# Attention on one Trainium2 core: value products split by key halves, scores tiled by two heads and 64 tokens

## The chip, the cores and the metric

The kernel runs on one core of a Trainium2 chip. The core has five engines that run side by side: TensorE (PE: matrix products; its weight loads are listed apart as PEld), VectorE (DVE), ScalarE (ACT), GpSimd (POOL) and SyncE (SP, which here only issues transfers). They meet in two on-chip memories: SBUF, with 128 partitions, and PSUM, where TensorE writes its results, in eight banks of 512 float32 numbers per partition. The metric is the device time of one execution in microseconds (us); lower is better.

## What is computed

Two layers over 1024 tokens of width 1024, in float32. The first is a gated MLP that mixes tokens in chunks of 128; it ends at about 640 us of the profile and is not touched. The second is sliding-window attention:

```python
logits = jnp.einsum('btkgd,bskd->bkgts', qb, kb).astype(jnp.float32) + alibi
valid = in_window & ((start - BLOCK + c) >= 0)        # 0 <= t - s < 128
logits = jnp.where(valid, logits, -jnp.inf)
m = jnp.maximum(jnp.max(logits, axis=-1), sink)
p = jnp.exp(logits - m[..., None])
denom = jnp.sum(p, axis=-1) + jnp.exp(sink - m)
o = jnp.einsum('bkgts,bskd->btkgd', p.astype(vb.dtype), vb).astype(jnp.float32)
o = o / denom.transpose(0, 3, 1, 2)[..., None]
y = out * jax.nn.silu(z)
return y @ w_out
```

There are 16 query heads of 64 channels in 4 groups; a group shares one key/value head. Tokens come in 8 blocks of 128. A token sees itself and the 127 tokens before it, so a block of queries needs the keys of its own block up to the token, and those of the block before it from the token on. Every token of a block thus has 128 keys with weight, spread over 256 keys.

## The kernel before

*Products in float32 from parts.* Long products use a split: a number is held as a rounded high part and a remainder (`split`, line 104; `mm3`, line 168), and three products (lines 169 to 171) stand for one. Scores and projections use this format (float32r). The value products and the transposes use plain float32 operands.

*A unit.* `Unit` (line 1041) is one block b of 128 queries for one pair p of key/value heads, so 8 query heads. There are 16 units. `scores(gp)` (line 1048) does half of a unit: two banks, one per head of the pair (`par`), each with two query heads side by side. For every query head and `par` it multiplies the query block (128 channels by 128 tokens; the high part stands in one half of the partitions, the remainder in the other) with the 256 keys, once with `kh` and once with `kl`: eight matmuls of 256 columns (line 1069). In block 0 there is no previous block and they have 128 columns. VectorE then folds the two key blocks into one: where the mask `mrg` (key index over token index) holds, the score of the current block is overwritten by that of the previous one (line 1074, 2 x 128 columns). It adds the slope bias and takes the maximum, with the sink as a lower bound, in one instruction per head (line 1080). ScalarE takes the exponential with its sum (line 1084). `normalise` divides. `transposes` (line 1092) turns the weights into keys by tokens with eight transposes (line 1097), ScalarE copies them to the tile `pc` (line 1098), and GpSimd cuts `pc` into the part of the previous block, `pp`, and that of the current block, `pc` (lines 1101, 1102).

*Value products.* `values` (line 1104) computes, for each `par`, 64 output channels by 512 columns (4 heads of 128 tokens): one matmul with the current block's values (`vt`, 128 keys by 64 channels, line 1116) and one with the previous block's (line 1118), added in the same bank `o`. The two `par` use the two column halves of the TensorE array. VectorE multiplies the bank with the gate (line 1122), and `split` writes the result over the queries, as the operand of the output projection.

*The order of work.* The attention is laid out by hand in `attn` (line 1125). In step i it issues `scores(0)` of unit i, `values` of unit i-2, two portions of filler, `transposes` of unit i-1, `scores(1)` and `normalise` of unit i, and two portions of filler. The filler (`more`) is a generator of other matmul work: key/value, query and gate projections of the second half of the tokens (`kv_phase`, `q_phase`, `z_phase`) during the first half's attention, and output projections (`out_b0`, `out_b1`) during the second's. Each engine runs its own instructions in the order given; semaphores are placed where a result of another engine is needed.

*Buffers.* PSUM has two rings of four banks. The ring "s" serves scores (two banks per group), `o` (one bank) and the transposes (two). Each use waits until the use four places earlier has been read out. `pc` and `pp` share a ring of two tiles in SBUF (tag "xt"). Small constants (`bias`, `mrg`, `qsc`, `snk`) are loaded by SP at line 945 on, and the sinks are negated by VectorE (line 957).

Of the kernel before, what the change touches and what calls it, by code (L numbers as in the profile page):

```python
# [14 lines left out]
P = 128  # L15
# [35 lines left out]
def tile_yoco(  # L51
# [891 lines left out]
    bp = ctx.enter_context(tc.tile_pool(name="bp", bufs=1))  # L943
    bias = bp.tile([P, 4, P], F32, name="bias")
    nc.sync.dma_start(out=bias.rearrange("p a b -> p (a b)"), in_=consts[:, C_BIAS:C_BIAS + 512])
    mrg = bp.tile([P, P], F32, name="mrg")
    nc.sync.dma_start(out=mrg, in_=consts[:, C_MERGE:C_MERGE + P])
    kh = [bp.tile([P, 2, S], F32R, name=f"kh{i}") for i in range(2)]
# [5 lines left out]
    nc.sync.dma_start(out=qsc, in_=consts[:, C_QS:C_QS + 2])  # L954
    snk = bp.tile([P, 4, 4], F32, name="snk")
    nc.sync.dma_start(out=snk.rearrange("p a b -> p (a b)"), in_=sinks.partition_broadcast(P))
    nc.vector.tensor_scalar(snk, snk, -1.0, None, ALU.mult)
    half = [slice(0, 64), slice(64, P)]
    vt = big.tile([P, NB, 256], F32, tag="P1_1", name="vt")
# [3 lines left out]
    def qz_four(h, which, m, n, evac):  # L963
# [3 lines left out]
        for kq in range(4):  # L967
            hi, lo = (t.rearrange("p (m k c) -> p m k c", m=4, k=2) for t in wnext())
            for i in range(4):
# [8 lines left out]
                yield  # L978

    def q_phase(h, n, q):  # L980
        def evac(m, ps):
            for par in range(2):
                rw = half[par]
                nc.scalar.activation(q[par][rw, m], ps[rw], AF.Copy, scale=qsc[rw, m // 4:m // 4 + 1])
            for par in range(2):
                rw, ot = half[par], half[1 - par]
                g = qsc[rw, m // 4:m // 4 + 1]
                nc.vector.scalar_tensor_tensor(q[par][ot, m], ps[rw], g, q[par][rw, m].bitcast(F32),
                                               ALU.mult, ALU.subtract)

        for m in range(0, 8, 4):
            yield from qz_four(h, 0, m, n, evac)
# [48 lines left out]
    class Unit:  # L1041
# [6 lines left out]
        def scores(self, gp):  # L1048
            b, p, q = self.b, self.p, self.q
            bs_ = slice((b % 4) * P, (b % 4 + 1) * P)  # L1050
            w0 = 0 if b > 0 else P
            if gp == 0:
                pr = bp.tile([P, 1088], F32, tag="pr", name=f"pr{self.id}", bufs=2)
                self.pr = pr = pr[:, 0:8 * (P + 1)].rearrange("p (a b) -> p a b", a=8)
                self.mx = bp.tile([P, 8], F32, tag="mx", name=f"mx{self.id}", bufs=2)
                self.dn = bp.tile([P, 8], F32, tag="dn", name=f"dn{self.id}", bufs=2)
                nc.vector.tensor_copy(pr[:, :, P].rearrange("p (c a b) -> p c a b", c=2, a=2),
                                      snk[:, 2 * p:2 * p + 2].rearrange("p a (c b) -> p c a b", c=2))
            pr, mx, dn = self.pr, self.mx, self.dn
            pss = []  # L1060
            for par in range(2):
                pss.append(bank("s", f"s{self.id}_{gp}{par}").rearrange("p (g s) -> p g s", g=2))
            ks = slice(b * P - P + w0, (b + 1) * P)

            for g in range(2):
                m = p * 4 + gp * 2 + g
                for par in range(2):
                    for k, w in enumerate((kh, kl)):
                        nc.tensor.matmul(pss[par][:, g, w0:256], lhsT=q[par][:, m, bs_], rhs=w[par][:, p, ks],  # L1069
                                         start=g + k == 0, stop=g + k == 2, skip_group_check=True)  # L1070
            for par in range(2):
                ps = pss[par]
                c = ps[:, :, P:256]
                nc.vector.copy_predicated(c, mrg.bitcast(U32).unsqueeze(1).broadcast_to([P, 2, P]),
                                          ps[:, :, 0:P] if b > 0 else neg.unsqueeze(1).broadcast_to([P, 2, P]))
                kv = 2 * p + par
                for g in range(2):
                    gg = 2 * gp + g
                    i = 4 * gp + 2 * par + g
                    nc.vector.tensor_tensor_reduce(pr[:, i, 0:P], c[:, g], bias[:, gg], -(4.0 ** -kv),  # L1080
                                                   snk[:, kv, gg:gg + 1], ALU.add, ALU.min, mx[:, i:i + 1])

            for i in range(4 * gp, 4 * gp + 4):
                nc.scalar.activation(pr[:, i], pr[:, i], AF.Exp, bias=mx[:, i:i + 1], scale=-1.0,  # L1084
                                     accum_out=dn[:, i:i + 1])
# [6 lines left out]
        def transposes(self):  # L1092
            self.pc = pc = st.tile([P, 8, P], F32, tag="xt", name=f"pc{self.id}")
            for gp in range(2):
                pt = bank("s", f"pt{self.id}_{gp}").rearrange("p (a b) -> p a b", a=4)
                for i in range(4):
                    nc.tensor.transpose(pt[:, i], self.pr[:, 4 * gp + i, 0:P], ident)
                nc.scalar.activation(pc[:, 4 * gp:4 * gp + 4], pt, AF.Copy)
            if self.b > 0:
# [4 lines left out]
        def values(self):  # L1104
            b, p, q, z = self.b, self.p, self.q, self.z
            bs_ = slice((b % 4) * P, (b % 4 + 1) * P)
            o = bank("s", f"o{self.id}")
            ov = o.rearrange("p (a b) -> p a b", a=2)
            for par in range(2):
                kv = 2 * p + par  # L1110
                vs = slice(kv * 64, kv * 64 + 64)

                def heads(w):
                    return w.rearrange("p (a b g) t -> p a b (g t)", a=2, b=2)[:, :, par]

                nc.tensor.matmul(ov[half[par]], lhsT=vt[:, b, vs], rhs=heads(self.pc), start=True, stop=b == 0)
                if b > 0:
                    nc.tensor.matmul(ov[half[par]], lhsT=vt[:, b - 1, vs], rhs=heads(self.pp),
                                     start=False, stop=True)
            ms = slice(p * 4, p * 4 + 4)  # L1120
            yt = z[p][:, :, bs_]
            nc.vector.tensor_tensor(yt, o.rearrange("p (a b) -> p a b", a=4), yt, ALU.mult)
            split(q[0][:, ms, bs_], q[1][:, ms, bs_], yt)

# [26 lines left out]
    def out_b0(y, yo, gp):  # L1151
        ss = const.tile([P, 2, 4], F32, tag="ss", name="ssb0")
        for gd in range(2):
            ps = [bank("mm", f"ob0_{gd}_{t}") for t in range(4)]
            for cp in range(4):
                hi, lo = wnext()
                for j in range(2):
                    m = 2 * cp + j
                    cs = slice(j * 512, j * 512 + 512)
                    for t in range(4):  # L1160
                        ts_ = slice(t * P, (t + 1) * P)
                        mm3(ps[t], y[0][:, m, ts_], y[1][:, m, ts_], hi[:, cs], lo[:, cs], m == 0, m == 7)
                        if t == 1:
                            yield
# [30 lines left out]
    def out_b1(y, yo, gp, ss0, yo0):  # L1195
        ss = const.tile([P, 2, 4], F32, tag="ss", name="ssb1")
        for gd in range(2):
# [5 lines left out]
            for t in range(4):  # L1203
                ps = bank("mm", f"ob1_{gd}_{t}")
                ts_ = slice(t * P, (t + 1) * P)
                for m in range(8):
                    mm3(ps, y[0][:, m, ts_], y[1][:, m, ts_], w[0][:, m], w[1][:, m], m == 0, m == 7)
                    if m % 2 == 1 and m < 7:
# [104 lines left out]
```

## Time and profile before

The time is the median of three runs, 1049.87 us (1049.35 to 1049.89).

| | before |
|---|---|
| profiled execution: span from first to last instruction | 1047.4 us |
| time of the runs, median | 1049.87 us |
| TensorE busy | 1038.3 us (99%) |
| VectorE busy | 732.1 us (70%) |
| ScalarE busy | 579.8 us (55%) |
| GpSimd busy | 187.0 us (18%) |
| attention stage | 766 to 1005 us |

The profile comes from one execution; its span is 2.5 us under the median of the runs, which is what lies ahead of the first and behind the last instruction it shows. A group line of the profile reads: source line, engine, operation, tiles written<-read, shape, count | busy us in total, mean ns of one | idle time of that engine just before them, and what ended it. A line of the order of time reads: start in us, length in us, engine, line, operation, tiles, shape, count. Matmuls are pipelined, so their lengths overlap; the distance between two starts is what one costs. A plain float32 matmul shows as two records.

### The profile page before, as it was taken

Reading aid. Unit: us, or ns where it says so; the run is one execution under the profiler, and the core shown is the slowest. Engines: PE = TensorE matmul, PEld = TensorE weight load, DVE = VectorE, ACT = ScalarE, POOL = GpSimd, SP = SyncE. Lnnn points to the kernel's source line nnn. Section 1 sums busy time; section 2 is a strip of 40 time slices with the busy share of each in tenths; the row PEclk is TensorE's granted clock in tenths of the full one; section 3 lists DMA queues with packets and bytes.
Section 4 is the critical chain, followed back from the end, with each engine's and each line's share of the span. In section 5 each row is a group of like instructions: output and inputs, shape, how many; then the busy total and the mean of one; then the engine's idle time right before and its main releaser. Section 6 shows DMA issues by size and latency. Waiting matters only on the chain.

```text
span 1047.4 us, 13677 instructions
## 1 busy us (share of the span) xinstructions
PE 1038.3 (99%) x4994; PEld 854.9 (82%) x4994; DVE 732.1 (70%) x1244; ACT 579.8 (55%) x998; POOL 187.0 (18%) x153
## 2 busy tenths in 40 slices
PE   9999999999999999999999999999999999999997
PEld 7888888888888888888888888888888777877776
DVE  6997467867768668677696587765247886667763
ACT  6694454555565565555444465654466665786631
POOL 0000003254342542530200000100001111021120
PEclk9999999999999999999999999999999999999999
DMA  8887252334333333337997643532222122211363
GB/s 309 271 287 268 101 181 84 118 109 142 120 121 116 133 124 117 105 137 271 324 352 276 200 163 94 201 102 89 94 79 71 52 81 62 80 61 62 121 221 120
DMA packets 80900, 157.56 MB, mean 150 GB/s; under 512 B 5825, under 2 KB 32705, under 8 KB 80833
## 3 DMA queue, kind: packets, MB, share of 16 engines
q1 hardware_dynamic: 76320, 148.01, 41.4%
q10 hardware_dynamic: 4512, 8.68, 2.4%
q8 instruction: 39, 0.64, 0.2%
q14 instruction: 29, 0.23, 0.1%
HBM read 125.21 MB, written 31.46 MB: 150 GB/s over the span
## 4 chain that ended last, share of the span: by engine, by line
PE 97%; DVE 1%; DMA 1%; ACT 1%; SPq 0%; issue 0%; DVEq 0%; POOLq 0%; ACTq 0%
PE ob L169 6%; PE qz L169 6%; PE ub L169 6%; PE ub L170 6%; PE ub L171 6%; PE qz L171 6%; PE ob L170 6%; PE ob L171 6%; PE qz L170 6%; PE s L1069 3%; PE uc L170 3%; PE uc L169 3%; PE uc L171 3%; PE sp L624 3%; PE vb L170 3%; PE vb L171 3%
## 5 line engine op out<-in xcount | busy, mean ns | idle before, releaser
L110 DVE SCALAR_TENSOR_TENSOR wlo<-raw_w,gn,whi 128x512 fp32r<-128x512 f32 x80 | 58.4, 758 | 62.2 <-ACT whi L109 62.0
L169 PE MATMUL qz<-n_hi,whi 128*128 128x512 f32 x256 | 100.9, 394 | 0.0
L171 PE MATMUL qz<-n_hi,wlo 128*128 128x512 f32 x256 | 99.8, 390 | 0.4 <-DVE wlo L110 0.4
L170 PE MATMUL qz<-n_lo,whi 128*128 128x512 f32 x256 | 99.9, 390 | 0.0
L109 ACT ACTIVATE whi<-raw_w,gn 128x512 fp32r<-128x512 f32 x80 | 54.7, 716 | 56.7 <-PE qz L170 36.5
L1084 ACT ACTIVATE pr<-pr,mx 128x129 f32<-128x129 f32 x128 | 50.1, 393 | 40.1 <-DVE mx L1080 40.0
L169 PEld LDWEIGHTS qz<-n_hi,whi 128*128 128x128 f32 x256 | 48.1, 188 | 15.8 <-issue 5.7
L105 ACT ACTIVATE uzhilo_g<-f 128x1024 fp32r<-128x1024 f32 x31 | 32.9, 1060 | 48.6 <-PE uc L171 42.7
L171 PEld LDWEIGHTS qz<-n_hi,wlo 128*128 128x128 f32 x256 | 48.0, 188 | 11.2 <-DVE wlo L110 0.9
L170 PEld LDWEIGHTS qz<-n_lo,whi 128*128 128x128 f32 x256 | 48.1, 188 | 9.3
L106 DVE TENSOR_TENSOR uzhilo_g<-f,uzhilo_g 128x1024 fp32r<-128x1024 f32 x31 | 39.0, 1259 | 19.8 <-ACT uzhilo_g L105 19.8
L209 ACT ACTIVATE uz_slots<-ub 128x512 f32<-128x512 f32 x48 | 28.3, 590 | 42.4 <-PE ub L171 39.1
L169 PE MATMUL ub<-T,whi_g 128*128 128x512 f32 x128 | 50.7, 396 | 0.0
L169 PE MATMUL ub<-T,uzhilo_g 128*128 128x512 f32 x128 | 50.5, 395 | 0.0
L171 PE MATMUL ub<-T,wlo_g 128*128 128x512 f32 x128 | 49.9, 390 | 0.0
L171 PE MATMUL ub<-T,uzhilo_g 128*128 128x512 f32 x128 | 49.9, 390 | 0.0
L170 PE MATMUL ub<-T,uzhilo_g 128*128 128x512 f32 x128 | 49.9, 390 | 0.0
L170 PE MATMUL ub<-T,whi_g 128*128 128x512 f32 x128 | 49.8, 389 | 0.0
L169 PE MATMUL uc<-T,uzhilo_g 128*128 128x512 f32 x124 | 48.9, 395 | 0.0
L170 PE MATMUL uc<-T,uzhilo_g 128*128 128x512 f32 x124 | 48.3, 389 | 0.0
L171 PE MATMUL uc<-T,uzhilo_g 128*128 128x512 f32 x124 | 48.3, 389 | 0.0
L105 ACT ACTIVATE whi_g<-raw_uz 128x1024 fp32r<-128x1024 f32 (+1 forms) x31 | 26.5, 854 | 37.1 <-PE ub L170 15.6
(334 smaller groups left out, 3066.9 us busy)
## 6 DMA issues: line engine op xcount, KB each, us to landing
raw_uz<-in_wuz_in_dram SPq DMA_DIRECT2D x32, 512.0 KB, 3.4
raw_w<-in_wqz_dram SPq DMA_DIRECT2D x32, 512.0 KB, 3.5
td<-uz_slots SPq DMA_DIRECT2D x56, 256.0 KB, 2.1
orawP2a<-td SPq DMA_DIRECT2D x28, 512.0 KB, 4.0
raw<-in_wv_in_dram SPq DMA_DIRECT2D x17, 512.0 KB, 4.8
vg<-vd SPq DMA_DIRECT2D x8, 1024.0 KB, 5.3
orawP2b<-in_wo_a_dram SPq DMA_DIRECT2D x16, 512.0 KB, 7.8
vraw<-in_wv_in_dram SPq DMA_DIRECT2D x13, 512.0 KB, 4.5
```

The costliest lines, as they stand in the source:

```text
L105: nc.scalar.activation(hi, src, AF.Copy)
L106: nc.vector.tensor_tensor(lo, src, hi.bitcast(F32), ALU.subtract)
L109: nc.scalar.activation(hi, src, AF.Copy, scale=g)
L110: nc.vector.scalar_tensor_tensor(lo, src, g, hi.bitcast(F32), ALU.mult, ALU.subtract)
L169: nc.tensor.matmul(out, lhsT=a_hi, rhs=b_hi, start=start, stop=False, skip_group_check=True)
L170: nc.tensor.matmul(out, lhsT=a_hi, rhs=b_lo, start=False, stop=False, skip_group_check=True)
L171: nc.tensor.matmul(out, lhsT=a_lo, rhs=b_hi, start=False, stop=stop, skip_group_check=True)
L209: nc.scalar.activation(out, a, AF.Copy)
L624: nc.tensor.matmul(psv[:, n], lhsT=d["vg"][:, 4 * j + n, i * P:(i + 1) * P], rhs=d["wc"], start=True, stop=True)
L1069: nc.tensor.matmul(pss[par][:, g, w0:256], lhsT=q[par][:, m, bs_], rhs=w[par][:, p, ks], start=g + k == 0, stop=g + k == 2, skip_group_che ...
L1084: nc.scalar.activation(pr[:, i], pr[:, i], AF.Exp, bias=mx[:, i:i + 1], scale=-1.0, accum_out=dn[:, i:i + 1])
```

## The change

- The scores take their stationary tile from two query heads by 64 tokens instead of one head by 128 tokens. For either token half `e` only three blocks of 64 keys can carry weight, so a matmul has 192 columns instead of 256 (64 and 128 in block 0). There are still eight per group. The first token half gets its key blocks in falling order, the second in rising order, so that one masked copy of 2 x 64 columns folds what was 2 x 128 (block 0 keeps the full one).
- For this the queries are stored with two heads side by side per 64 tokens (`by_half`), and the operand of the output projection with two heads side by side per 128 tokens (`by_head`). The constants `bias` and `mrg` are loaded in four pieces each instead of one, and the sinks through a helper tile.
- The value products of blocks 1 to 7 use tiles of 64 keys by 64 channels. Keys 0 to 63 go to the first bank: those of the current block for all tokens (512 columns), those of the previous block for the first 64 tokens of each head (256 columns). Keys 64 to 127 go to a second bank: those of the previous block for all tokens, those of the current block for the last 64. The key ranges left out have weight zero. Then ScalarE copies the first bank to SBUF, over `pc`, and VectorE adds the second. Block 0 keeps one bank and tiles of 128 keys.

```diff
+    half = [slice(0, 64), slice(64, P)]
+    bias = bp.tile([P, 2, 2, P], F32, name="bias")
+    mrg = bp.tile([P, 2, P], F32, name="mrg")
+    for e in range(2):
+        slopes = consts[half[e], C_BIAS:C_BIAS + 512].rearrange("r (a g j) -> g r a j", a=2, g=2)
+        for g in range(2):
+            nc.sync.dma_start(out=bias[half[g], :, e], in_=slopes[g])
+            nc.sync.dma_start(out=mrg[half[g], e], in_=consts[half[e], C_MERGE:C_MERGE + P])
...
+    sall = bp.tile([P, 4, 2, 2], F32, name="sall")
+    nc.sync.dma_start(out=sall.rearrange("p a b c -> p (a b c)"), in_=sinks.partition_broadcast(P))
+    snk = bp.tile([P, 2, 2, 2], F32, name="snk")
+    for g in range(2):
+        nc.vector.tensor_scalar(snk[half[g]], sall[half[g], :, :, g].rearrange("p (a c) b -> p a b c", a=2),
+                                -1.0, None, ALU.mult)
...
+    def by_half(t):
+
+        return t.rearrange("p k t -> p (k t)").rearrange("p (m b g r) -> p m b g r", m=4, g=2, r=64)
+
+    def by_head(t):
+
+        return t.rearrange("p k t -> p (k t)").rearrange("p (m b g t) -> p m b g t", m=4, g=2, t=P)
...
-            for g in range(2):
-                m = p * 4 + gp * 2 + g
+            for e in range(2):
+                n = 2 * b + e
                 for par in range(2):
+                    lhsT = by_half(q[par])[:, 2 * p + gp, 2 * (b % 4) + e].rearrange("p g r -> p (g r)")
                     for k, w in enumerate((kh, kl)):
-                        nc.tensor.matmul(pss[par][:, g, w0:256], lhsT=q[par][:, m, bs_], rhs=w[par][:, p, ks],
-                                         start=g + k == 0, stop=g + k == 2, skip_group_check=True)
+                        keys = w[par][:, p].rearrange("p (n r) -> p n r", r=64)
+                        if e == 0:
+                            keys = keys[:, n:n - 3:-1] if n > 2 else keys[:, n::-1]
+                            at = 0
+                        else:
+                            keys = keys[:, max(0, n - 2):n + 1]
+                            at = 192 if b > 0 else 256
+                        out = pss[par][:, at:at + 64 * keys.shape[1]].rearrange("p (n r) -> p n r", r=64)
+                        nc.tensor.matmul(out, lhsT=lhsT, rhs=keys,
+                                         start=e + k == 0, stop=e + k == 2, skip_group_check=True)
...
+                if b > 0:
+                    new = ps[:, 0:384].rearrange("p (a r) -> p a r", r=64)[:, 0:6:5]
+                    nc.vector.copy_predicated(new, mrg.bitcast(U32)[:, 0:1, 0:64].broadcast_to([P, 2, 64]),
+                                              ps[:, 128:256].rearrange("p (e r) -> p e r", e=2))
...
+            every, late = slice(0, P), half[1]
+            if b == 0:
+                first = [(slice(0, P), (self.pc, b, every), None)]
+            else:
+                first = [(half[0], (self.pc, b, every), (self.pp, b - 1, half[0])),
+                         (half[1], (self.pp, b - 1, every), (self.pc, b, late))]
+            os = [bank("s", f"o{self.id}_{i}") for i in range(len(first))]
+            for which in range(1 if b == 0 else 2):
+                for o, (rows, *parts) in zip(os, first):
+                    w, n, ts = parts[which]
+                    for par in range(2):
+                        vs = slice((2 * p + par) * 64, (2 * p + par) * 64 + 64)
+                        out = o.rearrange("p (a g t) -> p a g t", a=2, g=2)[half[par], :, :, ts]
+                        nc.tensor.matmul(out, lhsT=vt[rows, n, vs], rhs=heads(w, rows, par, ts),
+                                         start=which == 0, stop=b == 0 or which == 1, skip_group_check=True)
+            o = os[0]
+            if b > 0:
+                o = self.pc[:, 0:4].rearrange("p a t -> p (a t)")
+                nc.scalar.activation(o, os[0], AF.Copy)
+                nc.vector.tensor_tensor(o, os[1], o, ALU.add)
```

66 lines of the change are left out of this document (24 added, 42 removed).

## The prediction

> **What bounds the kernel now.** I read the page first (busy shares, slices, the chain that ended last), then the busy times of the attention stage by windows, then that stage's groups of instructions with their shapes kept apart, and last the instructions in order of time around single units.
>
> ```profile
> span 1047.4 us, 13677 instructions
> PE   9999999999999999999999999999999999999997
> PE 97%; DVE 1%; DMA 1%; ACT 1%; SPq 0%; issue 0%; DVEq 0%; POOLq 0%; ACTq 0%
> ...
> core 0: us, PE busy (x) PEld busy (x) DVE busy (x) ACT busy (x) POOL busy (x), PEclk, DMA share, GB/s
> 766.00:1005.00 239.00, 239.00 (x1266) 187.65 (x1265) 171.81 (x486) 159.50 (x421) 36.20 (x32) 1.00 0.23 74
> ```
>
> TensorE is busy in every slice and is 97% of the chain that ended last. The attention runs from 766 to 1005 us, mixed by hand with projection matmuls; there TensorE is busy 239.00 of 239.00 us at a granted clock of 1.00, VectorE 171.81 and ScalarE 159.50. So a microsecond taken from TensorE's stream there shortens the kernel by one, as long as no other engine's result comes late. The span is 1047.4 and the median of the runs 1049.87, so 2.5 us lie around the span; I take differences and put them on the median.
>
> **Value products: what changes on TensorE.** The groups of the stage, then one unit in order of time:
>
> ```profile
> L169 PE MATMUL qz<-n_hi,whi 128*128 128x512 f32 x130 | 51.9, 399 | 0.0
> L1116 PE MATMUL o<-pc,vt 128*64 128x512 f32 x64 | 17.4, 618 | 0.0
> L1118 PE MATMUL o<-pp,vt 128*64 128x512 f32 x56 | 14.5, 592 | 0.0
> ...
> 802.83 0.39 PE L169 MATMUL qz<-n_hi,whi 128*128 128x512 f32 x1
> ...
> 803.51 0.39 PE L169 MATMUL qz<-n_hi,whi 128*128 128x512 f32 x1
> ...
> 804.63 1.08 PE L1116 MATMUL o<-pc,vt 128*64 128x512 f32 x4
> 805.54 1.03 PE L1118 MATMUL o<-pp,vt 128*64 128x512 f32 x4
> 806.50 0.50 PE L169 MATMUL qz<-n_hi,whi 128*128 128x512 f32 x1
> ...
> 804.63 0.20 PEld L1116 LDWEIGHTS o<-pc,vt 128*64 128x64 f32 x4
> ```
>
> A unit with a previous block (14 of the 16) issues four value matmuls of 512 columns, and each shows as two records: 8 records from 804.63 to 806.50, 1.87 us. A 512-column matmul of the projections takes a third of 803.51 - 802.83 = 0.227 us; the score matmuls of 256 columns below step by 0.12, so a column costs (0.227 - 0.120)/256 = 0.42 ns and 512 cost 0.214 us. A float32 record is 592 ns long against 390 for the projections, 0.20 more, which is one more passage of 512 columns: I take one record as u = 2 x 0.214 = 0.428 us. Eight in a row would be 3.4 us, so they run two at a time, one for each column half: 4u = 1.71 us, and 0.16 us of changing over. The order says the same. The loop issues L1116 and L1118 for the one half, then both for the other; the trace has all four L1116 ahead of the L1118. So the halves take their work independently, and a record passes at least two earlier ones of the other half.
>
> The change makes four tiles of 64x64. Each does one matmul of 512 columns and one of 256: 2u + 2(u/2) = 3u if all four run at once, instead of 4u. That is 0.43 us less per unit, 14 x 0.43 = 6.0 us less. The two units of block 0 keep their tiles. The trace has nothing split by key rows. The bounds are the four at once (-6.0) and the two row halves in turn: 2 x 3u = 6u, +0.86 per unit, +12.0. I take -6.0: the column halves already run at once, the key halves read disjoint partitions and each has its own bank. Weight loads double to 16 of 64x64 per unit; now four load side by side within 0.20 us (last row), less than half a record, so I add nothing.
>
> [...]
>
> **Scores.** Per group there are still 8 matmuls, each of 192 columns instead of 256.
>
> ```profile
> 767.61 0.27 PE L1069 MATMUL s<-kh,q_lo 128*128 128x128 f32 x1
> 767.72 0.28 PE L1069 MATMUL s<-kl,q_lo 128*128 128x128 f32 x1
> 767.83 0.45 PE L169 MATMUL pk<-n_hi,whi 128*128 128x512 f32 x1
> 768.12 0.40 PE L170 MATMUL pk<-n_lo,whi 128*128 128x512 f32 x1
> ...
> 811.83 0.28 PE L1069 MATMUL s<-kh,q_lo 128*128 128x256 f32 x1
> 811.95 0.28 PE L1069 MATMUL s<-kl,q_lo 128*128 128x256 f32 x1
> ...
> 812.55 0.40 PE L169 MATMUL qz<-n_hi,whi 128*128 128x512 f32 x1
> 812.78 0.40 PE L170 MATMUL qz<-n_lo,whi 128*128 128x512 f32 x1
> ```
>
> 256 columns step by 0.12 us and 128 (block 0) by 0.11: half the columns save 0.008 us, because each matmul brings its own weight load. So 192 lie at 0.112 as well: 28 groups x 8 x 0.008 = -1.8 us. After the 128-column group the first long matmul is followed 0.29 us later (767.83 to 768.12) instead of 0.23 after a 256-column one; the same lag would come back in the 17 of 28 groups that value products don't follow: 17 x 0.06 = +1.0. I take -0.8. Bounds: columns alone (0.093 each) -6.0; 0.112 replaced by a load not hidden at all, 0.06 + 0.08 = 0.14, would be +4.5, though the 256 row denies it.
>
> **The work behind the values.** The two banks must be added: a ScalarE copy and a VectorE addition per unit.
>
> ```profile
> L1098 ACT ACTIVATE pc<-pt 128x512 f32<-128x512 f32 x32 | 17.3, 594 | 11.9 <-PE pt L1097 11.8
> L1122 DVE TENSOR_TENSOR z<-o,z 128x512 f32<-128x512 f32 x16 | 11.0, 686 | 4.2 <-PE o L1118 4.0
> L1074 DVE COPY_PREDICATED s<-mrg,s 128x256 f32<-128x256 uint32 x56 | 21.4, 424 | 14.5 <-PE s L1069 12.4 <-ACT pr L1084 1.9
> L1080 DVE CUSTOM_DVE_ANT_0 pr<-s,bias,snk 128x128 f32<-128x128 f32 x128 | 37.6, 347 | 0.2
> ```
>
> Copy like L1098: 14 x 0.594 = 8.3 us of ScalarE (159.5 to 168). Addition like L1122: 14 x 0.686 = 9.6 us of VectorE. The predicated copy falls to half its elements, between 0.21 (half of 424) and 0.35 (L1080); at 0.29 56 of them give back 7.5. VectorE 172 to 174, in about 232. Neither becomes the bound. What counts is when the second bank and the weights' buffer come free. In the unit above and in the tightest one:
>
> ```profile
> 807.55 0.69 DVE L1122 TENSOR_TENSOR z<-o,z 128x512 f32<-128x512 f32 x1
> 808.32 0.19 ACT L1084 ACTIVATION_READ_ACCUMULATOR pr<-pr,mx 128x1 f32 x1
> 811.43 1.09 ACT L1098 ACTIVATE pc<-pt 128x512 f32<-128x512 f32 x2 [2.40 <-PE pt L1097]
> 811.51 0.36 PE L1069 MATMUL s<-kh,q_hi 128*128 128x256 f32 x1
> ...
> 831.54 1.04 PE L1118 MATMUL o<-pp,vt 128*64 128x512 f32 x4
> 837.70 0.69 DVE L1122 TENSOR_TENSOR z<-o,z 128x512 f32<-128x512 f32 x1
> 838.47 0.19 ACT L1084 ACTIVATION_READ_ACCUMULATOR pr<-pr,mx 128x1 f32 x1
> 838.88 0.36 PE L1069 MATMUL s<-kh,q_hi 128*128 128x256 f32 x1
> 839.09 1.32 ACT L109 ACTIVATE whi<-raw_w,gn 128x512 fp32r<-128x512 f32 x2
> ```
>
> The copy is queued behind the four exponentials of the next scores (to 808.5), the addition follows it (809.1 to 809.8), the product ends at 810.5; TensorE wants those banks for the second score group at 811.5: one microsecond of slack. In the unit of 831 VectorE reaches the product only 5 us after the values (837.70); there the copy would end at 839.2 and the addition at 839.9, while the scores start at 838.9 and meanwhile TensorE has gained on VectorE: a wait of 0.7 to 2. Behind the waiting score matmul stand TensorE's projections, so it is lost. I add 1.0 for it and leave the other 13 at nothing. The weights' buffer, now also scratch for the sum, is free at 810.5, ahead of its next evacuation at 811.4. Query evacuations and the transposed evacuation write the same elements in runs of 64; ScalarE's and VectorE's idle quarter covers them.
>
> **Constants.** Two loads become eight.
>
> ```profile
> L945 SPq DMA_DIRECT2D bias<-in_consts_dram x1: 345/345/345, 638.8 to 638.8; - x1
> L956 SPq DMA_DIRECT2D snk<-in_sinks_dram x1: 430/430/430, 640.2 to 640.2; - x1
> snk<-in_sinks_dram SPq DMA_DIRECT2D x1, 8.0 KB, 2.6
> 643.34 0.16 DVE L957 TENSOR_SCALAR snk<-snk 128x16 f32<-128x16 f32 x1
> 647.80 0.75 DVE L110 SCALAR_TENSOR_TENSOR wlo<-raw_w,gn,whi 128x512 fp32r<-128x512 f32 x1 [3.49 <-ACT whi L109]
> ```
>
> Six more at about 0.45 us on SP's queue delay the sinks from 640.2 to 642.9; with 2.6 us to land, VectorE waits at its first use until 645.5 instead of 643.3. The weight split behind it slips by about 2.3 us, and VectorE idled 3.49 us ahead of 647.80: hidden, nothing added. Without that cover it would cost 2.
>
> **Sum:** -6.0 - 0.8 + 1.0 = -5.8: 1049.9 - 5.8 = 1044.1.
>
> **Rivals.**
> 1. *The row halves take turns* (the change doesn't do what it says). For: no row of this trace has two key halves at once. Against: column halves do, and the banks are separate. +12.0 - 0.8 + 1.0: 1062. [...]
> 2. *Pairs overlap but row halves are taken in program order.* The first pair of the second half starts one u late, the shorter ones queue: 4u in all, as before. -0.8 + 1.0: 1050. For: only passing within a pair of column tiles is seen.
> 3. *The longer chain stalls TensorE in every unit.* Place: the second score group waiting for the bank that the addition frees. It decides from (6.0 + 0.8)/14 = 0.49 us per unit on. The slack was one microsecond, and ScalarE can be behind by a weight split (1.32 us at 839.09); 1 us in each of 14 units gives 1049.9 - 6.8 + 14 = 1057. Against: most units have their product right behind the values, and TensorE waits for nothing now.
>
> **How the numbers follow.** Forecast 0.67, with its own range 1041.5 to 1047.5 (scores from -1.8 to nothing, waits from nothing to 4); rival 1 with the strict order 0.13, rival 2 0.12, rival 3 0.08. The range 1041.3 to 1052 holds the forecast, rival 2 and the mild end of rival 3, and leaves out 0.2. Within 0.2% (2.1 us, about what a measurement can tell from no change) is rival 2: 0.12. Faster 0.67, slower 0.21.
>
> **What would show it.** Right: per unit the value records start four together, twice 0.43 and twice 0.21 apart, and the next projection starts 1.44 us after the first; score matmuls of 192 columns step by 0.112; no wait of TensorE for the addition but around the fourth unit. Wrong: value records spread over 2.5 us or more (rival 1), 1.87 us as now (rival 2), or gaps ahead of the second score group (rival 3); a step of 0.14 or more between score matmuls would upset the second term.

## The result, and the profile after

The changed kernel is slower. Its median is 1056.16 us (1054.28 to 1057.07, 4 runs) against 1049.88 (1049.35 to 1050.48, 4 runs): ratio 1.0059, 95% interval 1.0046 to 1.0071. The forecast was 1044.1. The profiled execution spans 1054.5 us, 7.1 more than before.

From the page of the changed kernel, and then its attention stage by windows (the columns are those of the prediction's window row):

```profile
PE   9999999999999999999999999999999999989997
PEclk9999999999999999999999999999999999999899
PE 83%; DVE 6%; ACT 5%; DMA 3%; issue 2%; POOL 1%; SPq 0%; DVEq 0%; POOLq 0%; ACTq 0%
```

```profile
766.00:1005.00 239.00, 233.45 (x1347) 185.61 (x1346) 172.90 (x495) 166.44 (x432) 33.34 (x30) 0.99 0.22 71
```

TensorE's share of the chain that ended last fell from 97% to 83%. VectorE (172.90 against 171.81) and ScalarE (166.44 against 159.50) are hardly busier. So no engine became the bound; TensorE now waits. One of the late slices shows it busy for less than 90%, and another a granted clock below 0.9.

What TensorE was to save, it saves. A unit's value products in order of time (start, length, engine, line, operation):

```profile
805.17 0.65 PE L1152 MATMUL o<-pc,vt 64*64 64x512 f32 x2
805.18 0.65 PE L1152 MATMUL o<-pp,vt 64*64 64x512 f32 x2
805.65 0.59 PE L1152 MATMUL o<-pc,vt 64*64 64x512 f32 x2
...
806.09 0.38 PE L1152 MATMUL o<-pc,vt 64*64 64x256 f32 x2
806.29 0.38 PE L1152 MATMUL o<-pp,vt 64*64 64x256 f32 x2
...
806.62 0.50 PE L169 MATMUL qz<-n_hi,whi 128*128 128x512 f32 x1
```

Four records start together (two `pc`, two `pp`), then steps of 0.48, 0.44 and 0.20; the next projection starts 1.45 us after the first record, where it was 1.87. The groups behind the values, on VectorE and ScalarE from 766 to 1010 us, and what TensorE waited for in the whole execution:

```profile
L1099 DVE COPY_PREDICATED s<-mrg,s 128x128 f32<-128x128 uint32 x56 | 15.7, 292 | 2.6 <-PE s L1092 2.4
L1157 ACT ACTIVATE pc<-o 128x512 f32<-128x512 f32 x13 | 7.6, 584 | 6.7 <-PE o L1152 6.6
L1158 DVE TENSOR_TENSOR pc<-o,pc 128x512 f32<-128x512 f32 x13 | 9.0, 691 | 17.8 <-ACT pc L1157 17.8
```

```profile
PE o L1152 <- POOL pc L1129: 2.9, 2, 1.5
PE o L1152 <- DVE mx L1106: 1.5, 1, 1.5
...
PE s L1092 <- ACT pc L1157: 1.0, 1, 1.0
PE qz L169 <- DVE q_lo L1004: 0.8, 1, 0.8
...
PE s L1092 <- DVE pc L1158: 0.3, 1, 0.3
```

The new operations cost what the prediction said (292, 584 and 691 ns). But VectorE stands idle 17.8 us waiting for the copy. And TensorE, which waited for nothing in this stage before, now waits 6.5 us, in six waits. They lie near 833, 925, 934, 979 and 1006 us.

The largest place is the unit at 978.6. TensorE, VectorE and ScalarE there, in order of time:

```profile
978.60 1.07 PE L1152 MATMUL o<-pc,vt 64*64 64x512 f32 x4
981.22 1.89 PE L1152 MATMUL o<-pp,vt 64*64 64x512 f32 x8 [1.55 <-DVE mx L1106]
...
983.90 0.79 PE L169 MATMUL ob<-whi,q_hi 128*128 128x512 f32 x1
```

```profile
979.31 1.23 DVE L106 TENSOR_TENSOR wob_lo<-raw_ob,wob_hi 128x1024 fp32r<-128x1024 f32 x1 [0.83 <-ACT wob_hi L105]
980.45 0.35 DVE L1106 CUSTOM_DVE_ANT_0 pr<-s,bias,snk 128x128 f32<-128x128 f32 x1
```

```profile
978.22 1.06 ACT L105 ACTIVATE wob_hi<-raw_ob 128x1024 fp32r<-128x1024 f32 x1 [2.34 <-DMA raw_ob<-in_wo_b_dram]
979.18 0.39 ACT L1110 ACTIVATE pr<-pr,mx 128x129 f32<-128x129 f32 x1
```

Read backwards: the bank that the second half of the products is to be written to still holds scores, which the score reductions (L1106) read. Those stand in VectorE's queue behind `wob_lo`, the remainder of an output-projection weight. That waits for `wob_hi` on ScalarE, which waits 2.34 us for the transfer that brings the weight. The unit takes 5.3 us (978.60 to 983.90) instead of 1.45, and its second half and the projections behind it run at half clock. The windows give the clock (third column from the end):

```profile
982.00:984.00 2.00, 2.00 (x11) 0.69 (x5) 1.88 (x3) 1.77 (x6) 0.00 (x0) 0.50 0.52 203
984.00:988.00 4.00, 4.00 (x10) 3.13 (x11) 3.49 (x12) 1.49 (x7) 0.00 (x0) 0.50 0.66 206
```

The projections there step by 0.43 us (985.34 to 985.77) instead of 0.23 (988.27 to 988.50), so by my estimate from these steps the six microseconds at half clock are about three lost.

Why is a weight split ahead of the exponentials at all? It wasn't in the kernel before. ScalarE there, at the same point:

```profile
974.05 0.39 ACT L1084 ACTIVATE pr<-pr,mx 128x129 f32<-128x129 f32 x1
974.43 2.01 ACT L105 ACTIVATE wob_hi<-raw_ob 128x1024 fp32r<-128x1024 f32 x2
```

Four exponentials first, then two weight splits that wait for nothing. The change doesn't touch these lines. The order in which ScalarE, VectorE and GpSimd take their work is laid out anew when a kernel is built, and the diff shows nothing of it. The same happened on GpSimd: the last `pc` is cut only at 1006.55, because two powers of the output norm now stand between the cut of `pp` and that of `pc`:

```profile
1002.87 1.09 POOL L1128 TENSOR_SCALAR_AFFINE_SELECT pp<-pc 128x1024 f32<-128x1024 f32 x1 [8.68 <-ACT pc L1125]
1003.93 2.66 POOL L1221 TENSOR_TENSOR ef<-ef,small 128x1 f32<-128x1 f32 x2
1006.55 1.70 POOL L1129 TENSOR_SCALAR_AFFINE_SELECT pc<-pc 128x1024 f32<-128x1024 f32 x1
```

### The profile page after: what moved, and what is told of

Same layout as the page of the kernel before. It is cut to its first block, busy times and chain, and to the rows that moved or that the text cites. A ratio compares the mean times of both kernels' runs of the same rounds, so it can differ in the third digit from the quotient of the medians.

```text
span 1054.5 us, 13950 instructions
## 1 busy us (share of the span) xinstructions
PE 1038.2 (98%) x5106; PEld 856.0 (81%) x5106; DVE 738.4 (70%) x1259; ACT 588.1 (56%) x1012; POOL 186.9 (18%) x153
## 4 chain that ended last, share of the span: by engine, by line
PE 83%; DVE 6%; ACT 5%; DMA 3%; issue 2%; POOL 1%; SPq 0%; DVEq 0%; POOLq 0%; ACTq 0%
PE ub L169 6%; PE ub L171 6%; PE ub L170 6%; PE ob L169 5%; PE qz L169 5%; PE ob L171 5%; PE ob L170 5%; PE qz L171 4%; PE qz L170 4%; PE uc L170 3%; PE uc L169 3%; PE uc L171 3%; PE sp L624 3%; PE oc L169 2%; PE oc L171 2%; PE oc L170 2%
```

## The experiments

Two theories at first. A: the longer chain (copy, addition, product) holds the banks and is the loss. B: the loss is the new order in the queues, weight splits and powers ahead of attention work. All times below are medians; each ratio is against the kernel before on the same chip, with its 95% interval.

### The change in parts

`scores_only` takes the new scores, layouts and constants and keeps the old `values`. `values_only` is the other half. `no_sum` is the changed kernel without copy and addition; it takes the first bank alone, so the weights of keys 64 to 127 are left out of its output:

```diff
             o = os[0]
-            if b > 0:
-                o = self.pc[:, 0:4].rearrange("p a t -> p (a t)")
-                nc.scalar.activation(o, os[0], AF.Copy)
-                nc.vector.tensor_tensor(o, os[1], o, ALU.add)
             nc.vector.tensor_tensor(yt, o.rearrange("p (a b) -> p a b", a=4), yt, ALU.mult)
```

`dve_sum` keeps the whole change but reads both banks on VectorE:

```diff
-                o = self.pc[:, 0:4].rearrange("p a t -> p (a t)")
-                nc.scalar.activation(o, os[0], AF.Copy)
-                nc.vector.tensor_tensor(o, os[1], o, ALU.add)
+                part = self.pc[:, 0:4]
+                nc.vector.tensor_tensor(part, os[0].rearrange("p (a b) -> p a b", a=4), yt, ALU.mult)
+                nc.vector.tensor_tensor(yt, os[1].rearrange("p (a b) -> p a b", a=4), yt, ALU.mult)
+                nc.vector.tensor_tensor(yt, part, yt, ALU.add)
```

Expected of scores_only:

> Only the scores, the stored order of the queries and the constants are changed; the value products are those of before. Theory A (the copy and the addition behind the second bank hold banks and the weights' buffer until TensorE waits): no loss without them, 1048 to 1050 us, TensorE without a gap over 0.3 us in the attention. Theory B (any change of the costs in this stage makes the planner order the queues of ScalarE, VectorE and GpSimd another way, so that weight splits which wait for a transfer stand ahead of attention work): a loss of 2 to 6 us also here.

Expected of values_only:

> Only the value products are changed (64x64 tiles in two banks, copy and addition); scores and constants are those of before. Theory A: the whole loss is here, 1055 to 1058 us. Theory B: the loss depends on the order that the planner happens to make, anything from 1044 to 1060, with the waits at other units than in the changed kernel.

Expected of no_sum:

> The changed kernel without the ScalarE copy and the VectorE addition: only the first bank is used, so the weights of keys 64 to 127 are left out of the output; TensorE has the same matmuls. Theory A: the saving of TensorE comes through, 1042 to 1045 us. Theory B: the waits behind weight splits and GpSimd's small power stay, 1047 to 1055 us.

Expected of dve_sum:

> The changed kernel with both banks multiplied by the gate on VectorE and the two products added there: no ScalarE copy, the first bank is free one VectorE instruction after the values, the second after two; VectorE has one instruction of 0.69 us more per unit instead of the copy. Theory A: about half of the loss is gone, 1045 to 1050 us. Theory B: no rule, 1044 to 1058.

| | us | ratio |
|---|---|---|
| scores_only | 1049.64 | 1.0002 (0.9993 to 1.0011) |
| values_only | 1050.00 | 1.0002 (0.9993 to 1.0012) |
| no_sum | 1049.94 | 0.9999 (0.9989 to 1.0009) |
| dve_sum | 1051.77 | 1.0021 (1.0011 to 1.0030) |

Each half alone changes nothing that can be measured, and with no chain at all the kernel still gains nothing. A alone falls: it had expected 1055 to 1058 of `values_only`, 1042 to 1045 of `no_sum` and 1045 to 1050 of `dve_sum`. In `scores_only` the total fits A, but TensorE waits 1.6 us in the attention, once for 0.9, where A had expected no gap over 0.3. In the trace of `no_sum` the values save their 0.42 us per unit, but one unit at 973.8 takes 4.9 us, behind the same weight split, and half clock follows it (0.50 in the windows from 979 to 981). Before anything could be said of the change, the orders had to be held.

### Two orders held

`hold_` kernels pin two orders and change nothing else in the program; what they don't name may still move. ScalarE takes the four weight splits of the first output half behind named exponentials of the last units, and GpSimd's powers stay in the order of the program:

```diff
+    def behind(ins, other):
+        tc.add_manual_dep(ins.ins, other.ins.name, mybir.DependencyInfo(
+            mybir.DependencyClass.NoSync, mybir.DependencyReason.DATA), reason="hold")
...
-        nc.gpsimd.tensor_tensor(r, r, nhalf[:, 0:1], ALU.pow)
+        tc.keep_in_program_order(nc.gpsimd.tensor_tensor(r, r, nhalf[:, 0:1], ALU.pow))
...
-                split(wv[0][:, cp], wv[1][:, cp], raw)
+                whi = nc.scalar.activation(wv[0][:, cp], raw, AF.Copy)
+                if gd == 0:
+                    behind(whi, exps[((6, 1, 0), (6, 1, 1), (6, 1, 1), (7, 1, 0))[cp]])
+                nc.vector.tensor_tensor(wv[1][:, cp], raw, wv[0][:, cp].bitcast(F32), ALU.subtract)
```

Expected of hold_before, the control:

> The kernel before with the same two orders pinned: the control. Its TensorE waits for nothing in the attention and its exponentials already stand ahead of most of those splits, so both theories expect 1049.6, within 1. A gain of more than 1.5 here would mean that the pins help whatever the change.

Expected of hold_after:

> The changed kernel with two queue orders pinned and nothing else altered: ScalarE takes the four splits of the output-projection weights for columns 0 to 511 (L106, wob_hi) only behind the exponentials of units (block 6, pair 1) and (7, 1), and GpSimd takes the powers of the output norm (L1221) in program order, behind the last cuts of pc. Theory B (the order in the queues eats the gain): the 3.85 us of TensorE in the unit at 978.6, the half-clock stretch behind it (some 2 us) and the 1.6 us at 1006.5 go; 1056.2 - 7.5 = about 1048.7, 1047 to 1051, and no steps of 0.43 us between 512-column matmuls in 975 to 995. Theory A (the longer chain of copy and addition is the loss): those waits sit in the banks, so at least 1054 remains.

Expected of hold_no_sum:

> The kernel without copy and addition (the second bank, so the weights of keys 64 to 127, is left out of the output), with the same two orders pinned. Theory B: the 3.5 us lost in the unit at 973.8 and the half-clock stretch behind it (1.2 us) go, the TensorE saving of 6 us then shows: 1044 to 1046.5. Theory A: without the chain there was nothing left to lose, so it stays at 1049.9 within 1.

Expected of hold_values_only:

> Old scores and constants, new value products with copy and addition, the two orders pinned. Theory B: the values' waits for GpSimd's cut at 987 and 999 (0.9 + 1.6 us) go: 1047.5, 1046.5 to 1048.5. Theory A: no wait there comes from the order, 1050 stays.

Expected of hold_scores_only, which ran in a later group:

> New scores, layouts and constants, old value products, the two orders pinned. The kernel without the addition and with the orders pinned was 6.4 us under the kernel before with them pinned; this splits that sum. If the score term is worth -0.8 as predicted, 1048.6 (1047.8 to 1049.2) and the values carry 5.6 to 6; if the scores' share is -1.8 or more, 1047.6 or less; if the new layouts cost as much as they save, 1049.4.

| | us | ratio |
|---|---|---|
| hold_before | 1049.42 | 1.0002 (0.9993 to 1.0010) |
| hold_scores_only | 1047.34 | 0.9980 (0.9972 to 0.9989) |
| hold_values_only | 1047.89 | 0.9984 (0.9975 to 0.9993) |
| hold_no_sum | 1043.01 | 0.9940 (0.9928 to 0.9953) |
| hold_after | 1052.94 | 1.0033 (1.0022 to 1.0044) |

The control doesn't move; the changed kernel gains 3.2 us and `no_sum` 6.9. With the orders held, the scores are worth 2.1 us (1049.42 to 1047.34) and the values without their addition another 4.3 (to 1043.01): 6.4 together. That is the saving that the prediction had put at 6.8; 1043.01 is below the 1044 to 1046.5 that had been expected of `hold_no_sum`. TensorE's only wait for the values there:

```profile
PE o L1157 <- POOL pc L1134: 0.4, 1, 0.4
```

But `hold_after` missed its expectation of 1047 to 1051: adding the two banks costs 9.9 us there. So neither theory is whole. B is right on 3.2 us, and the larger part shows only with A's chain in place. Where it costs, `hold_after` shows at 933 us; ScalarE, then VectorE, then TensorE:

```profile
929.53 1.06 ACT L1021 ACTIVATE z<-z 128x1024 f32<-128x1024 f32 x1
930.60 1.28 ACT L1115 ACT_TABLE_LOAD   x1
931.89 0.41 ACT L1115 ACTIVATE pr<-pr,mx 128x129 f32<-128x129 f32 x1
...
933.45 0.57 ACT L1162 ACTIVATE pc<-o 128x512 f32<-128x512 f32 x1
```

```profile
934.06 0.69 DVE L1163 TENSOR_TENSOR pc<-o,pc 128x512 f32<-128x512 f32 x1 [3.10 <-ACT pc L1162]
```

```profile
934.08 0.36 PE L1097 MATMUL s<-kh,q_hi 128*128 128x192 f32 x1 [0.99 <-ACT pc L1162]
...
934.80 0.36 PE L1097 MATMUL s<-kh,q_lo 128*128 128x192 f32 x1 [0.26 <-DVE pc L1163]
```

VectorE is free 3.1 us earlier. The copy, though, is queued on ScalarE behind a Silu, a table load and four exponentials, and the second score group waits for both banks.

This price isn't a fixed sum, though. The row of `hold_values_only` says so: with the old scores, the new values and their addition together gain 1.5 us, so there the addition costs 2.8 if the values save the same 4.3. The largest place of `hold_after` shows one reason. ScalarE there, and then ScalarE in `hold_values_only` at the same point:

```profile
984.31 1.04 ACT L1245 ACTIVATE wob_hi<-raw_ob 128x1024 fp32r<-128x1024 f32 x1
985.26 0.57 ACT L1162 ACTIVATE pc<-o 128x512 f32<-128x512 f32 x1
```

```profile
981.56 0.58 ACT L1135 ACTIVATE pc<-o 128x512 f32<-128x512 f32 x1
982.05 1.06 ACT L1218 ACTIVATE wob_hi<-raw_ob 128x1024 fp32r<-128x1024 f32 x1
```

The hold keeps this weight split behind the exponentials, but it doesn't say whether the split or the copy comes first. In `hold_after` the split does, and VectorE too takes the weight's remainder ahead of the addition. TensorE waits 1.07 and 0.92 us there, and 3.4 us of half clock follow (0.50 in the window from 988 to 990.5): by my estimate, the two waits and half of the 3.4, some 3.7 of the 9.9 us. In `hold_values_only` the copy comes first, and TensorE waits for neither copy nor addition there. So part of the 9.9 is again an order that the change doesn't name. No run holds this split behind the copy, so how much of the 9.9 would be left stays open.

`wob_after` tells the two orders apart:

> The changed kernel with only the weight splits (L106, wob_hi) held behind the exponentials; GpSimd's powers stay where the planner puts them, two of them between the last two cuts. If the powers cost the 1.6 us of the wait at 1006.5, this comes out 1.6 above the kernel with both orders pinned (1052.9): 1054.5. If that wait has other slack to fall into: 1053.

It measured 1052.93 (1.0039, 1.0025 to 1.0053), the same as with both held. Holding the powers brought nothing that can be measured, although the wait they cause is back in its trace. The profile of `hold_after` has 3.4 us of half clock from 987.2 on that the one of `wob_after` hasn't (0.67 against 1.00 in the window from 988 to 992). By my estimate, half of the 3.4, that is a loss of about as much as that wait; whether it is the other side of the sum stays open.

### The copy taken off ScalarE, or moved

Theory C from here: what is left is the place of the chain in queues. D: holding two banks costs, whoever reads them. `hold_dve_sum` is the VectorE sum of above with the orders held; `hold_vfirst` issues `values` ahead of the first score group in `attn`; `hold_vfirst_dve` does both:

```diff
-            if i < len(units):
-                units[i].scores(0)
             if 0 <= i - 2:
                 units[i - 2].values()
+            if i < len(units):
+                units[i].scores(0)
```

Expected of hold_dve_sum:

> The changed kernel with the two orders pinned and without the ScalarE copy: VectorE multiplies both banks with the gate and adds the products, so nothing behind the values passes through ScalarE's queue. Theory C (beside the orders, what is lost is the place of the copy in ScalarE's queue, behind four exponentials, and around 930 behind a weight split, two table loads and a Silu): the waits of the second score group at 932.8 and 984.5 (1.6 and 2.3 us) and the half clock behind the latter (1.5) shrink to under 1 us together: about 1048, 1046.5 to 1049.5. Theory D (two banks held at all are the loss, whoever reads them; VectorE's 1.4 us more per unit): 1052 or more, as in the kernel with the orders pinned alone (1052.9).

Expected of hold_vfirst:

> The changed kernel with the two orders pinned and, in each step of attn, values of unit i-2 issued ahead of the first score group of unit i instead of behind it. Copy and addition then stand ahead of the four exponentials and the reductions of that group in both queues. Theory C: waits for the banks go except around 930, where Silu still stands ahead of the copy: 1047 to 1050. Against it: the values come some 0.9 us earlier, so that the wait for GpSimd's cut at 924.5 (1.5 us) grows to 2.4. Theory D: no gain, 1052.9 or more.

Expected of hold_vfirst_dve:

> Both of these together: VectorE reads both banks, and the values come ahead of the first score group, the two orders pinned. Theory C: the least waits of the three, 1044.5 to 1047.5, faster than the kernel before (1049.5) and 1.5 to 4 above the kernel without the addition (1043.0). Theory D: 1052 or more.

| | us | ratio |
|---|---|---|
| hold_dve_sum | 1048.19 | 0.9988 (0.9979 to 0.9997) |
| hold_vfirst | 1054.46 | 1.0047 (1.0033 to 1.0061) |
| hold_vfirst_dve | 1059.59 | 1.0095 (1.0082 to 1.0109) |

Reading both banks on VectorE gains 4.7 us over `hold_after`, although VectorE then works 186.3 us in the stage instead of 172.9 in the changed kernel. D falls on this row. The move was a clear miss: I had counted on 2 to 5 us, and lost 1.5 and 11.4. The longest waits in `hold_vfirst`:

```profile
PE s L1097 <- DVE mx L1111: 2.8, 3, 1.6
PE o L1157 <- POOL pc L1134: 2.7, 1, 2.7
```

The wait for the cut was foreseen (2.4 expected, 2.7 measured). Not foreseen: the reductions of the first score group now stand behind addition, product and split in VectorE's queue, and the second score group waits for their banks. Half clock follows as well: 3.4 us behind the wait for the cut in `hold_vfirst` (928.5 to 931.9), and two such stretches in `hold_vfirst_dve` (in one, 0.50 in the windows from 996 to 999; the mean granted clock of the two executions is 0.998 and 0.996).

### The wait that was left

In `hold_dve_sum` the values wait for GpSimd's cut at 925 and 988, 1.3 us each (1.4 and 1.5 counted from start to start). At the second place, ScalarE, GpSimd and TensorE:

```profile
985.85 0.63 ACT L105 ACTIVATE q_hi<-z 128x512 fp32r<-128x512 f32 x1 [1.89 <-DVE z L1164]
986.38 1.07 ACT L1130 ACTIVATE pc<-pt 128x512 f32<-128x512 f32 x2
```

```profile
988.73 1.09 POOL L1134 TENSOR_SCALAR_AFFINE_SELECT pc<-pc 128x1024 f32<-128x1024 f32 x1
```

```profile
989.87 0.65 PE L1157 MATMUL o<-pc,vt 64*64 64x512 f32 x2 [1.28 <-POOL pc L1134]
```

ScalarE stands idle 1.89 us for the last link of the chain, because the split of the finished output (`q_hi`) is queued ahead of the evacuation of the next transposes. `hold_dve_late` holds that split behind the evacuation in every step, `hold_dve_two` in the third and the eighth step of the second half only; `before_late` and `before_two` do the same to the kernel before:

```diff
+            held = h == 1 and i in (2, 7)
             if 0 <= i - 2:
                 units[i - 2].values()
+                if not held:
+                    units[i - 2].finish(None)
...
                 units[i].normalise()
+            if held:
+                units[i - 2].finish(units[i - 1].evac)
...
+        def finish(self, evac):
+            whi = nc.scalar.activation(hi, src, AF.Copy)
+            if evac is not None:
+                behind(whi, evac)
+            nc.vector.tensor_tensor(lo, src, hi.bitcast(F32), ALU.subtract)
```

Expected of hold_dve_late and its control:

> As the kernel with the orders pinned and the sum on VectorE (1048.2), and in each step the split of the finished output (q_hi on ScalarE, q_lo on VectorE) is issued behind the second score group and held, on ScalarE, behind the evacuation of the next unit's transposes. Theory C (what the change loses is queue order behind the longer chain): the values' waits for GpSimd's cut at 925.1 and 988.2 (1.4 + 1.5 us) go: 1045.5, 1044.5 to 1046.8. Theory D (the second bank itself costs the rest): 1048 stays.

> The control: the kernel before with the two orders pinned and the same split moved and held. Its TensorE waits for nothing in the attention, so 1049.4, within 1.

Expected of hold_dve_two and its control:

> As the kernel with the orders pinned and the sum on VectorE (1048.2), with the split of the finished output held behind the evacuation of the next unit's transposes in two steps only, the third and the eighth of the second half of the tokens, where the values waited 1.4 and 1.5 us for GpSimd's cut. Theory C: both waits go and no new one of over 1 us comes: 1045.8, 1045 to 1047. Theory D: 1048 stays, or another wait takes their place.

> The control: the kernel before with the two orders pinned and the same split held in the same two steps. No wait stands there, so 1049.4, within 1.

| | us | ratio |
|---|---|---|
| hold_dve_late | 1049.95 | 1.0008 (0.9999 to 1.0017) |
| before_late | 1052.44 | 1.0030 (1.0018 to 1.0041) |
| hold_dve_two | 1045.44 | 0.9965 (0.9951 to 0.9979) |
| before_two | 1049.50 | 1.0001 (0.9993 to 1.0010) |

Held everywhere, the two waits shrank to 0.5 and 0.2 us, but the split then blocked other work, and both kernels missed what was expected of them. In `hold_dve_late` VectorE took the remainder `q_lo` ahead of the evacuation of an output bank (this is the top row of TensorE's waits there), and the control lost 3.0 us too:

```profile
PE ob L169 <- DVE yb L1230: 2.6, 1, 2.6
```

Held where the waits stood, it gave 1045.44, inside its expectation, and the control didn't move. `hold_dve_two` beats both kernels. What TensorE still waits for there in the attention:

```profile
PE s L1097 <- DVE z L1163: 1.2, 2, 0.8
...
PE o L1157 <- POOL pc L1134: 0.5, 1, 0.5
PE o L1157 <- DVE mx L1111: 0.3, 1, 0.3
```

The series with orders held adds up the case. Its differences belong to this order of the steps; `hold_values_only` shows that another order gives others:

| step | us | difference |
|---|---|---|
| kernel before | 1049.42 | |
| new scores | 1047.34 | -2.1 |
| new values, no addition | 1043.01 | -4.3 |
| both banks added through VectorE, split held in two steps | 1045.44 | +2.4 |
| split where it was put | 1048.19 | +2.8 |
| first bank through ScalarE | 1052.94 | +4.7 |
| orders as laid out: the changed kernel | 1056.16 | +3.2 |

The rows come from several groups of runs; the kernel before stood between 1049.31 and 1049.53 in all but the last row's, where it was 1049.88.

## Why the prediction was wrong

*What bounds the kernel.* "A microsecond taken from TensorE's stream there shortens the kernel by one, as long as no other engine's result comes late" holds (6.4 us of 6.8 in `hold_no_sum`). The condition in its second half was then hardly examined. The full TensorE row showed that nobody was late before. It didn't show by how little.

*Value products.* Right. The four tiles run at once: 1.45 us a unit for the 1.44 predicted. The term was -6.0; in the trace of `hold_no_sum` thirteen units save 5.4 in all, the fourteenth waits 0.4 us for GpSimd's cut and saves nothing, and -4.3 came out of the runs. Another 0.4 is a wait for `q_lo` elsewhere; the rest of the gap stays open. Rivals 1 and 2 are excluded by the rows at 805.17 and 805.18. No run shows the strict order that stands beside rival 1's chance: the first records of the four tiles start within 0.01 us, and a unit takes 1.45 us.

*Scores.* Right in kind, mis-sized: -2.1 for -0.8. The step is the 0.112 predicted, but the first projection behind a group is followed after 0.26 us (892.53 to 892.79), not the 0.29 taken over from the 128-column group; 0.23 stood there before. Some 0.02 us in 17 places are 0.4 of the +1.0. And a group, from its first matmul to what follows it, takes 0.08 us less in the traces with orders held, 2.3 in 28 groups for the 1.8 predicted. Together that is -1.9, near the -2.1 measured. The rows, from `hold_scores_only` in order of time:

```profile
892.42 0.27 PE L1097 MATMUL s<-kl,q_lo 128*128 128x192 f32 x1
892.53 0.41 PE L169 MATMUL qz<-n_hi,whi 128*128 128x512 f32 x1
892.79 0.40 PE L170 MATMUL qz<-n_lo,whi 128*128 128x512 f32 x1
```

*The work behind the values.* This is the step that failed: "I add 1.0 for it and leave the other 13 at nothing". The durations were right to 0.01 us. The price was not in them but in where they queue, and it was 9.9 us with the two orders held (2.8 with the old scores). The slack was read in the units at 805 and 831, both in the first half, and carried over to fourteen. The second half has other neighbours: Silu with its table loads near 930 (1.28 us each in `hold_after`), weight splits of the output projection near 980. Near 930 the copy came 3 us after VectorE was free for the addition. Two links that I priced at nothing each blocked something I didn't name. One is the split of the finished output, which became late by the length of the chain and stood ahead of the transposes' evacuation, and so of GpSimd's cut (2.8 us). The other is the copy itself, ahead of which ScalarE had whatever came up, at 984 the weight split (4.7 us). "ScalarE's and VectorE's idle quarter covers them" compares busy sums, and a sum says nothing on a queue.

*What no step had.* The prediction took the orders of ScalarE and GpSimd as fixed. They were laid out anew, with weight splits ahead of exponentials, worth 3.2 us in the changed kernel and 6.9 in the one without the addition.

*Constants.* The eight loads are hidden, as predicted: VectorE waits 3.9 us for the sinks, to 649.0, which is 3.5 later than the 645.5 worked out, but the attention of `hold_scores_only` begins at 767.06 against 766.99 before.

*Rival 3* (1057 by a microsecond in each of 14 units) has nearly the measured time, and its place, the second score group waiting for the bank, is one of those found. Its account is wrong all the same: most of the fourteen units lose nothing, and the loss sits in five places with different causes.

## What to carry to other kernels

When TensorE is full and an edit lengthens the chain behind it, look up what stands ahead of each new instruction in its engine's queue at every repetition, and what stands behind the instruction that becomes late. One repetition, or the sums of busy time, don't show it. Compare the order of all engines before and after an edit, since work that the diff doesn't touch may have moved, and hold the orders when the edit itself is to be measured, with the same hold on the unchanged kernel as control. Then look in the trace at what the hold left free. A price found so belongs to the queues that it was measured in; it needn't add up with others.

## What the runs showed of the hardware

Plain float32 products in four tiles of 64x64 run at once: a unit's 16 records took 1.45 us in the changed kernel, where 8 records in two column halves took 1.87 in the kernel before. The first records of all four tiles start within 0.01 us.

The granted clock fell to half after short waits. In the changed kernel two starts 2.13 us apart (979.09 to 981.22), with 1.55 us of idle time between them, were followed by it, and the granted clock was 0.50 from 981.35 to 988.18. In `hold_after`, waits of 1.07 and 0.92 us close together were followed by it, while the same pair in `wob_after` (the longest are 1.0 and 0.9) was not. The half clock lasted 6.83 us in the changed kernel, twice 3.41, and 3.4 (987.2 to 990.6) in `hold_after`; the full clock behind the step of the changed kernel lasted to 1053.03, 64.85 us or 19 times 3.41. So I laid stretches of 3.41 us over the two pairs; where they begin in `wob_after`, which has no step there, is my estimate. They tell the pairs apart (`hold_after`, then `wob_after`; the first number behind the length is TensorE's busy time):

```profile
983.82:987.23 3.41, 1.46 (x11) 1.05 (x9) 1.83 (x2) 2.01 (x6) 0.00 (x0) 1.00 0.52 198
```

```profile
983.00:986.42 3.42, 2.45 (x15) 1.89 (x14) 1.50 (x10) 3.06 (x10) 0.00 (x0) 1.00 0.90 286
986.42:989.83 3.41, 2.42 (x14) 2.03 (x15) 2.68 (x4) 1.27 (x4) 0.00 (x0) 1.00 0.51 150
```

In `hold_after` both waits fall into one stretch, which is left with 1.95 us idle, and the next runs at half clock. In `wob_after` a border between two stretches parts the waits, 0.97 and 0.99 us idle, and the clock stays at 1.00. In the changed kernel the stretch ahead of the step (977.94 to 981.35) has 1.65 us of TensorE idle; the other stretches at full clock from 766 to 1008.66, laid off from the same border, have 1.43 or less, and no step follows them. In `hold_vfirst` a wait of 2.66 us stands ahead of the step at 928.5. Why the half clock of the changed kernel lasts twice 3.41 us, though TensorE is busy for all of the first (3.41 of 3.41 from 981.35 to 984.76), stays open, and no run moved a pause on purpose.
